# A hybrid mixer and mixture-of-experts layer on one core: ten tiles of the last norm finished through TensorE and ScalarE, the first tokens' numbers loaded by SyncE, five routing steps folded

## The chip, the cores and the metric

The kernel runs on one core of a Trainium2 chip. The metric is the device time of one execution in microseconds (us). A run's page and trace come from one profiled execution; the times in the result come from executions of the same program.

## What is computed

The reference is one layer over 2048 latent tokens (D = 1024) with 256 context tokens: adaLN, a projection, an mLSTM head group and an RWKV-7 head group in both directions, an output projection and a layer norm; then a mixture of experts, and a last layer norm. The change lies in the last two parts:

```python
x   = layernorm(ALPHA * x + g1 * (mixed @ w_out), ln1_g, ln1_b)
h   = modulate(x, sh2, sc2)                      # (2048, 1024)
# per token: best group of 4, best two of its 8 experts, softmax weights
y   = (silu(h @ ex_gate[e]) * (h @ ex_up[e])) @ ex_down[e]   # 32 experts, width 512
out = layernorm(ALPHA * x + g2 * ffn, ln2_g, ln2_b)
```

The last line is, for each token, `(x - mean) * rs * ln2_g + ln2_b`, where rs is one over the root of the variance plus 1e-6. All inputs and outputs are float32.

## The kernel before

The program is one TileContext. A planner simulates the program when it is built and fixes the order of the instructions on each engine from that simulation; on the chip every engine then runs its own list strictly in that order and waits where an operand is missing. `issue_after(ins)` (used with `with`) keeps the instructions of its block behind `ins`, on the engine of `ins` only.

**Output projection and routing** (`out_proj`, `route`, `route_end`). Sixteen tiles of 128 tokens are projected, normed and modulated; the modulated rows go to the DRAM tensor H2, the normed rows to ACC. The logits of the tiles are routed in batches of 4, 4, 3, 3, 1 and 1 tiles (`BATCHES`). `route` (line 1405 on) is a chain of small VectorE (DVE) instructions: the group's maximum, its number `gi` as the smallest index where the logit equals the maximum (an index minus 16, and plus 16 again at L1424), the same twice for the experts (an index minus 64, plus 64 at L1435; a one-hot row `e` at L1436, copied into the bfloat16 table `OH` at L1437), then the rank of each token within its expert by two TensorE products of `OH` with constant matrices, a place number `pos = expert * 2048 + rank` (L1461), cast to integers at L1463, and one indirect DMA of GpSimd (POOL) per tile and choice that writes token number and weight into the DRAM table TB (L1477): 32 scatters in all, ten of them in the last three batches.

**Experts** (`moe`). Every matrix of an expert is loaded as float32 in pieces (tile `eraw`, L1518, SyncE's queue) and split into a high part `eH` (ScalarE, L1531) and a rest `eL` (DVE, L1532: eraw minus eH), 12 pieces of 128x1024 per expert; the products run as three float32r matmuls each (L1565). `AHEAD = 8` pieces of the first expert are split before the tokens' numbers are asked for, two more (`W += ...`, line 1706) at the head of the loop over the 32 experts, the last two inside `gate_up`. Around the first tokens the order is:

- `load_ids(ids0, ...)`: a small DMA on POOL's queue (L1577) reads the numbers of the first 128 tokens of experts 0 and 1 from TB; it waits for all 32 scatters.
- `fetch` and `gather`: POOL's indirect DMAs (L1582) fetch the rows of H2: expert 0's tokens into `xg`, expert 1's into a tile of the weights' pool. The first weights of expert 1 wait for the second gather.
- `load_ids(t, ...)`: a second small DMA on POOL's queue loads the numbers for all experts into `yo`; POOL casts them (L1670).
- `split_T`: TensorE (PE) transposes `xg` (L1540), ScalarE takes the high part (L1548), DVE the rest (L1553); the last of these DVE instructions is `order`. Then PE transposes `t` in two halves (L1680), DVE copies each into `ids` (L1681), and expert 0's gate product begins.

The loop then runs 32 experts, adds each result into ACC with an accumulating scatter of POOL (L1651), and hands over to the last norm.

**Last norm** (`finish`). All 16 tiles of ACC are loaded (L1784). For tiles with m % 8 in (1, 3, 5, 6) ScalarE forms mean and variance with two passes (L1792, L1793), for the others DVE does (bn_stats, L75); DVE subtracts the mean and multiplies by ln2_g (L1796 or L1799), then multiplies by rs and adds ln2_b (L1800), both over 128x1024. The tile is stored from SyncE's queue (L1801).

Of the kernel before, what the change touches and what calls it, by code (L numbers as in the profile page):

```python
# [8 lines left out]
F = mybir.dt.float32  # L9
FR = mybir.dt.float32r  # L10
BF = mybir.dt.bfloat16
I32 = mybir.dt.int32
# [10 lines left out]
SEQ = 2048  # L23
# [15 lines left out]
def raw(ap, offset, dims):  # L39
    return bass.AP(tensor=ap.tensor, offset=ap.offset + offset, ap=dims)  # L40
# [13 lines left out]
class Kern:  # L54
# [4 lines left out]
    def pool(self, name, bufs, **k):  # L59

        if k.get("space") is not DRAM:
            k["reuse_waits"] = "tile"
        return self.tc.tile_pool(name=name, bufs=bufs, **k)
# [1313 lines left out]
    def route_consts(self, cp):  # L1377
        nc = self.nc
        c32 = cp.tile([128, 2, 32], I32, name="ci32")
        nc.gpsimd.iota(c32[:, 0, :], pattern=[[1, 32]], base=0, channel_multiplier=0)  # L1380
        nc.gpsimd.iota(c32[:, 1, :].rearrange("p (g e) -> p g e", e=8), pattern=[[1, 4], [0, 8]], base=0, channel_multiplier=0)
        self.i32 = cp.tile([128, 2, 32], F, name="cf32")
        nc.vector.tensor_copy(self.i32, c32)
        tk = cp.tile([128, 16], I32, name="tokid")
        nc.gpsimd.iota(tk, pattern=[[128, 16]], base=0, channel_multiplier=1)
        self.tokid = tk
        o = cp.tile([128, 128], F, name="onesf")
        nc.gpsimd.memset(o, 1.0)
        self.ones_b = cp.tile([128, 128], BF, name="ones_b")
        nc.vector.tensor_copy(self.ones_b, o)  # L1390
        nc.gpsimd.affine_select(out=o, in_=o, compare_op=OP.is_gt, fill=0.0, base=0, pattern=[[1, 128]],
                                channel_multiplier=-1)
        self.tri_b = cp.tile([128, 128], BF, name="tri_b")
        nc.vector.tensor_copy(self.tri_b, o)
        self.scat = []
        self.cnt = cp.tile([128, 32], F, name="cnt")
        nc.vector.memset(self.cnt, 0.0)
        self.OH = cp.tile([128, 16, 2, 32], BF, name="OH")
        self.rank = cp.tile([128, 16, 2], F, name="rank")
        self.keep = {}  # L1400
        for n2 in sorted(set(2 * n for _, n in BATCHES)):
            k = self.keep[n2] = cp.tile([128, 32, n2], F, name="keep%d" % n2)
            nc.vector.memset(k, 1.0)
            nc.vector.memset(k[:, :, 0:1], 0.0)

    def route(self, m0, n, L, rp, pp):
# [2 lines left out]
        bc = lambda a, w: a[:, :, None].to_broadcast([128, n, w])  # L1409
        row = lambda a: a[:, None, :].to_broadcast([128, n, a.shape[-1]])  # L1410
        lg, le = L[:, :, 0:4], L[:, :, 4:36]
        i32, grp = self.i32[:, 0, :], self.i32[:, 1, :]
        sm = rp.tile([128, 7, n], F, name="rsm%d" % n)
        gm, gi, i1, i2, v1, v2, pg = (sm[:, i, :] for i in range(7))
        b4 = rp.tile([128, n, 4], F, name="rw4%d" % n)
# [5 lines left out]
        nc.vector.tensor_scalar(b4, a4, 0.0, None, op0=OP.is_equal)  # L1421
        nc.vector.scalar_tensor_tensor(b4, b4, -16.0, row(i32[:, 0:4]), op0=OP.mult, op1=OP.add)
        nc.vector.tensor_reduce(gi, b4, axis=AX.X, op=OP.min)
        nc.vector.tensor_scalar(gi, gi, 16.0, None, op0=OP.add)  # L1424
        x = rp.tile(S, F, name="rx%d" % n)
        e = rp.tile(S, F, name="re%d" % n)
        nc.vector.tensor_tensor(e, row(grp), bc(gi, 32), op=OP.is_equal)
# [2 lines left out]
        for j, (v, i) in enumerate(((v1, i1), (v2, i2))):  # L1430
            nc.vector.tensor_reduce(v, x, axis=AX.X, op=OP.max)
            nc.vector.tensor_tensor(e, x, bc(v, 32), op=OP.is_equal)
            nc.vector.scalar_tensor_tensor(e, e, -64.0, row(i32), op0=OP.mult, op1=OP.add)
            nc.vector.tensor_reduce(i, e, axis=AX.X, op=OP.min)
            nc.vector.tensor_scalar(i, i, 64.0, None, op0=OP.add)  # L1435
            nc.vector.tensor_tensor(e, row(i32), bc(i, 32), op=OP.is_equal)  # L1436
            nc.vector.tensor_copy(self.OH[:, ms, j, :], e)  # L1437
            if j == 0:
                nc.vector.scalar_tensor_tensor(x, e, -2e30, x, op0=OP.mult, op1=OP.add)
        oh = self.OH[:, ms].rearrange("p i j e -> p (i j e)")  # L1440
        n2 = 2 * n
        ps = pp.tile([128, 2, n2, 32], F, name="rps")
# [17 lines left out]
        for j, i in enumerate((i1, i2)):  # L1460
            nc.vector.scalar_tensor_tensor(pos[:, :, j], i, float(SEQ), self.rank[:, ms, j], op0=OP.mult, op1=OP.add)  # L1461
        pi = rp.tile([128, n, 2], I32, name="rpi%d" % n)
        nc.vector.tensor_copy(pi, pos)  # L1463

        en = rp.tile([128, n, 2, 2], I32, name="ren%d" % n)
        nc.vector.tensor_copy(en[:, :, :, 0], self.tokid[:, ms][:, :, None].to_broadcast([128, n, 2]))
# [30 lines left out]
    def moe(self):  # L1497
        tc, nc, I, s = self.tc, self.nc, self.I, self.scratch
        with ExitStack() as es:
# [73 lines left out]
                                  mybir.DependencyInfo(mybir.DependencyClass.Sync, mybir.DependencyReason.DATA),  # L1573
                                  reason=reason)

            def load_ids(dst, src):
                ld = nc.gpsimd.dma_start(dst, src)  # L1577
                for sc in self.scat:
                    behind_dma(ld, sc, "entries of the token table")

# [76 lines left out]
                return x  # L1657

            Rs = {0: load_raw(0)}
            W = [split(Rs[0], i) for i in range(AHEAD)]  # L1660
            ids0 = ap.tile([128, 2, 2], I32, name="ids0", bufs=1)
            load_ids(ids0, raw(TBf, 0, [[2, 128], [2 * SEQ, 2], [1, 2]]))
            x0 = fetch(ids0[:, 0, 0:1])
            x = rawp.tile([128, 4, 512], F, name="eraw").rearrange("p k c -> p (k c)")[:, 0:D]
            self.first = gather(x, ids0[:, 1, 0:1])

            t = xp.tile([128, D], F, name="yo", bufs=1)[0:32, 0:768]
            load_ids(t.bitcast(I32), raw(TBf, 0, [[2 * SEQ, 32], [1, 768]]))
            t = t.rearrange("p (i w) -> p w i", w=2)
            nc.gpsimd.tensor_copy(t[:, 0], t[:, 0].bitcast(I32))  # L1670
            self.scat = []
# [25 lines left out]
            for e in range(NE):  # L1697
                nx, x1 = coming

                with behind():  # L1700
                    tc.mark_branch_hint_location("e%d" % e, hint=nx, engines=[PE])
                cur = ids[:, 0, e]
                act = bp.tile([128, DE], F, name="act")
                Aa = parts(bp, 4, "a")
                us = [pu.tile([128, 512], F, name="epu%d" % h) for h in range(2)]
                W += [split(Rs[e], i) for i in range(len(W), 10)]
                if left:
                    add(*left)
                with behind() if e == 0 else ExitStack():
                    gate_up(X, W, Rs[e])  # L1710
                last = self.pe

                def extra(i):


                    if not isinstance(i, int) or i > 1:
                        new = ap.tile([128, 2], I32, name="more")
                        load_ids(new, self.TB[bass.ds((i + (16 * e + 1)) * 128, 128), :])
                        gather(x1, new[:, 0:1])
                    else:  # L1720
                        new = ids[:, 1 + i, e]
                    old = ap.tile([128, 2], I32, name="old")
                    nc.vector.tensor_copy(old, cur)
                    nc.vector.tensor_copy(cur, new)
                    self.pe = None
                    Z = parts(xp, 8, "z")

                    def mid():
                        with tc.If(nx > 1):
                            gather(x1, ids[:, 2, e, 0:1])  # L1730

                    add(tail(W, lambda g: split_T(Z, x1, g, 4, later=g == 0), mid if isinstance(i, int) and i == 0 else None), old)
                    gate_up(Z, W)

                if e + 1 < NE:
                    coming = begin(e + 1, order)
                with tc.If(nx > 0, label="e%d" % e):  # L1737
                    tc.mark_branch_hint_location("f%d" % e, hint=nx - 1, engines=[PE])
                    extra(0)
                    with tc.If(nx > 1, label="f%d" % e):  # L1740
                        extra(1)
                        with tc.If(nx > 2):
                            with tc.For_i(2, nx, 1) as i:
                                extra(i)

                def fill(g):
                    nonlocal x
                    if e + 1 < NE:
                        late = split_T(X, x, g, 4, True, last, g == 0)
                    else:  # L1750
                        late = None
                    if g == 1 and e + 2 < NE:
                        x = fetch(ids[:, 0, e + 2, 0:1])
                    return late

                self.pe = None
                X = parts(xp, 8, "x")
                left = tail(W, fill), cur
                order = self.last
                if e + 2 < NE:  # L1760
                    Rs[e + 2] = load_raw(e + 2)
                if e + 1 < NE:
                    W = [split(Rs[e + 1], i) for i in range(2)]
                    with tc.issue_after(self.evac[0]), tc.issue_after(self.evac[1]):
                        W += [split(Rs[e + 1], i) for i in range(2, AHEAD)]
            add(*left)

    def finish(self):
        tc, nc, I = self.tc, self.nc, self.I
        with ExitStack() as es:  # L1770
# [2 lines left out]
            l2g, l2b = rows[:, 0], rows[:, 1]  # L1773
            for x, nm in ((l2g, "ln2_g"), (l2b, "ln2_b")):
                nc.scalar.dma_start(x, self.bcast_rows(flat(I[nm]), D))
            xp, tp = pool("fx", 8), pool("ft", 4)

            nc.scalar.activation(tp.tile([128, 1], F, name="fsq", bufs=1), self.eps_ln, AF.Sqrt)
            xs = []
# [5 lines left out]
            sq = tp.tile([128, D], F, name="fsc", bufs=1)  # L1785
            for m in range(16):
                x = xs[m]
                if m % 8 in (1, 3, 5, 6):

                    st = tp.tile([128, 4], F, name="fst")  # L1790
# [6 lines left out]
                else:  # L1797
                    mu, rs = self.ln_stats(tp, x, D, LN_EPS, "f")
                    nc.vector.scalar_tensor_tensor(x, x, mu, l2g, op0=OP.subtract, op1=OP.mult)  # L1799
                nc.vector.scalar_tensor_tensor(x, x, rs, l2b, op0=OP.mult, op1=OP.add)  # L1800
                nc.sync.dma_start(self.out[0, 128 * m:128 * m + 128], x)  # L1801

    def run(self, stop=None):
# [46 lines left out]
```

## Time and profile before

| | us |
|---|---|
| runs | 3412.34, 3418.94, 3422.70 (median 3418.94) |
| profiled execution, its own time | 3418.58 |
| its span, first to last instruction | 3417.0 |
| first gate product of expert 0 starts | 2306.65 |
| last product of the experts ends | 3351.4 |
| first and last DVE instruction of the last norm | 3361.99 and 3411.79 (ends 3413.07) |

Times in the rows are us from the start of the span. The execution's own time is 1.6 us longer than its span; the sum of the prediction is made against the execution's own time, 3418.58, which lies 0.36 us under the median. A row of the timeline view gives start, duration, engine, line, operation, written and read tiles, and in brackets how long the engine had been idle and what released it. DVE instructions overlap by some 0.1 us, so that the distance of two starts is the price of one in a row of them, not the duration. [...]

### The profile page before, as it was taken

To read this page: it belongs to the slowest core of one execution; us is meant where nothing else is said; L and a number is where in the kernel's file an instruction comes from. 1 tells how busy PE (TensorE), PEld (TensorE's weight loads), DVE (VectorE), ACT (ScalarE), POOL (GpSimd) and SP (SyncE) were. 2 spreads that over 40 slices of the span, in tenths; PEclk is the share of its full clock that TensorE was granted. 3 is DMA by queue.
4 is the path that set the end of the run, shared out by engine and by line. 5 is a ranking of instruction groups with operands and counts; after the bars stand their busy time and mean duration, and the time that the engine had idled before them with its cause. 6 is when DMAs were issued, how large, how long until landed. Compare 5 with 4: busy or idle time off the path is not lost. (4 is left out here: it accounts for less than half of the span.)

```text
span 3417.0 us, 61401 instructions
## 1 busy us (share of the span) xinstructions
PE 2866.9 (84%) x24042; PEld 2405.9 (70%) x24042; DVE 2339.6 (68%) x3822; ACT 1364.0 (40%) x2187; POOL 879.0 (26%) x862
## 2 busy tenths in 40 slices
PE   6899999999979964777777588859899989989992
PEld 3677788898757754666666567647778877878781
DVE  4488888766787875667656288875877736476447
ACT  4432322335545322334344233344655525355233
POOL 5400000013455660112112365431222212122210
PEclk9899999999979875778788789979999999999996
DMA  5333332235468534666664554448988848597535
GB/s 187 117 114 108 101 116 82 88 101 189 164 219 242 167 109 115 171 159 170 155 168 128 159 174 137 141 147 286 334 295 284 304 125 276 159 335 234 177 112 209
DMA packets 471689, 602.59 MB, mean 176 GB/s; under 512 B 127222, under 2 KB 312338, under 8 KB 471314
## 3 DMA queue, kind: packets, MB, share of 16 engines
q1 hardware_dynamic: 413617, 441.15, 41.2%
q0 software_dynamic: 36736, 129.33, 13.0%
q10 hardware_dynamic: 20960, 27.20, 2.5%
q8 instruction: 224, 3.67, 0.5%
q14 instruction: 152, 1.24, 0.1%
HBM read 453.24 MB, written 144.33 MB: 175 GB/s over the span
## 5 line engine op out<-in xcount | busy, mean ns | idle before, releaser
L1532 DVE TENSOR_TENSOR eL<-eraw,eH 128x1024 fp32r<-128x1024 f32 x384 | 449.6, 1221 | 28.6 <-ACT eH L1531 24.6
L329 DVE SCALAR_TENSOR_TENSOR cacc<-P,cw,cacc 128x1008 f32<-128x1008 f32 (+3 forms) x320 | 398.7, 1247 | 56.5 <-ACT cacc L304 45.6
L1531 ACT CAST eH<-eraw 128x1024 fp32r<-128x1024 f32 x384 | 370.9, 1052 | 48.3 <-PEq L1737 35.1
L263 PE MATMUL in_ps<-hH,w_H 128*128 128x512 f32 (+1 forms) x664 | 252.3, 382 | 1.7 <-ACT pl_ev L355 1.7
L263 PE MATMUL in_ps<-hL,w_H 128*128 128x512 f32 (+1 forms) x664 | 249.6, 377 | 0.0
L263 PE MATMUL in_ps<-hH,w_L 128*128 128x512 f32 (+1 forms) x664 | 248.0, 374 | 0.0
L1565 PE MATMUL epo<-eH,aH 128*128 128x512 f32 x408 | 172.2, 422 | 64.8 <-DVEq L1737 32.2
L1651 POOL DMA_INDIRECT ACC<-yo,ids x32 | 131.0, 4093 | 250.5 <-DVE yo L1650 226.1
L1565 PE MATMUL epo<-eH,aL 128*128 128x512 f32 x408 | 159.7, 404 | 11.7 <-DVE aL L1553 11.7
L1565 PE MATMUL epo<-eL,aH 128*128 128x512 f32 x408 | 163.2, 400 | 0.0
L931 PE MATMUL rpg<-KR,BK 64*128 64x128 f32 (+1 forms) x1152 | 122.4, 350 | 46.7 <-ACT BT L941 17.5
L237 POOL DMA_DIRECT2D w_raw<-in_w_in x28 | 21.2, 757 | 506.2 <-DVE w_L L251 371.8
L263 PEld LDWEIGHTS in_ps<-hH,w_H 128*128 128x128 f32 x664 | 126.2, 191 | 34.6 <-issue 11.5
L931 PEld LDWEIGHTS rpg<-KR,BK 64*128 64x128 f32 x1152 | 104.9, 248 | 63.2 <-issue 23.8
L973 DVE TENSOR_TENSOR sT<-sM,sY 128x31 f32<-128x31 f32 (+15 forms) x279 | 95.3, 342 | 78.8 <-DMA sM<-BL 70.8
L298 ACT COPY P<-in_ps 128x512 f32<-128x512 f32 (+1 forms) x92 | 51.3, 557 | 235.8 <-PE in_ps L263 235.8
L1565 PE MATMUL epu<-eH,xL 128*128 128x256 f32 x512 | 143.4, 283 | 0.0
L1565 PE MATMUL epu<-eL,xH 128*128 128x256 f32 x512 | 143.2, 283 | 0.0
L263 PEld LDWEIGHTS in_ps<-hL,w_H 128*128 128x128 f32 x664 | 126.2, 190 | 22.7 <-issue 2.1
L1565 PE MATMUL epu<-eH,xH 128*128 128x256 f32 x512 | 142.2, 288 | 0.0
L263 PEld LDWEIGHTS in_ps<-hH,w_L 128*128 128x128 f32 x664 | 126.1, 190 | 22.3 <-issue 0.8
L1565 PEld LDWEIGHTS epo<-eH,aH 128*128 128x128 f32 x408 | 78.9, 193 | 83.1 <-ACT xH L1548 30.7
(471 smaller groups left out, 8151.1 us busy)
## 6 DMA issues: line engine op xcount, KB each, us to landing
eraw<-in_ex_gate SPq DMA_DIRECT2D x64, 1024.0 KB
eraw<-in_ex_up SPq DMA_DIRECT2D x64, 1024.0 KB
eraw<-in_ex_down SPq DMA_DIRECT2D x64, 1024.0 KB
pk<-PK SPq DMA_DIRECT2D x144, 320.0 KB
PK<-pk POOLq DMA_DIRECT2D x36, 768.0 KB, 3.9
ada_w<-in_w_ada SPq DMA_DIRECT2D x32, 512.0 KB
v<-MV SPq DMA_DIRECT2D x50, 264.0 KB
kc<-KTd SPq DMA_DIRECT2D x50, 256.0 KB
```

What stands on the lines that cost most here:

```text
L237: self.wld = nc.gpsimd.dma_start(w[:, 4:8, o:o + cn], src[:, 4:8])
L263: nc.tensor.matmul(o, a[:, k, :], b, start=i == 0, stop=i == 3 * KT - 1)
L298: nc.scalar.copy(P[:, t0:t0 + n], ps)
L329: nc.vector.scalar_tensor_tensor(o, img[:, r0 + sy:r1 + sy, c0 + sx:c1 + sx], wt(dy, dx), o, op0=OP.mult, op1=OP.add)
L931: nc.tensor.matmul(pG[e][:, q, b.cols], b.BK[HD[e], c, q, :], b.KR[HD[e], c, q, b.cols], start=True, stop=True, tile_position=(64 * e, 0))
L973: nc.vector.tensor_tensor(tt, M[:, 0:j, j:j + 1].to_broadcast([128, j, w]), Y[:, j:j + 1, j:32].to_broadcast([128, j, w]), op=OP.mult)
L1531: self.cp = nc.scalar.copy(H, w)
L1532: nc.vector.tensor_tensor(L, w, H, op=OP.subtract)
L1565: self.pe = nc.tensor.matmul(o, a[:, k, :], b[:, kw, c], start=first and i == 0, stop=last and i == 2)
L1651: nc.gpsimd.indirect_dma_start(out=self.ACC, out_offset=bass.IndirectOffsetOnAxis(ap=cur[:, 0:1], axis=0), in_=y, in_offset=None, compute_ ...
```

## The change

Four edits. In `route` the indices stay at minus 16 and minus 64: the constants they are compared with are lowered by as much once (two more small DVE instructions in `route_consts`), the one-hot row is written straight into `OH`, and the place number is corrected by 64 * 2048 in the integer cast. So five DVE instructions of every batch go (one of L1424, two of L1435, two of L1437). In `moe` both `load_ids` before the loop go to SyncE's queue; only six pieces are split ahead, and the other four up to ten are traced at the head of the loop behind `order`, on DVE. In `finish`, for the ten tiles with m % 8 in (1, 2, 4, 5, 6), L1800 is replaced: POOL scales the identity by rs into `fdg` (128x128), PE adds the bias row as a product of a row of ones (`one`, K = 1) with ln2_b and the scaled tile as a product with `fdg`, per half of 512 columns, in one PSUM accumulation (tiles `fps`, three of them, two banks each), and ScalarE copies the 128x1024 sum to SBUF.

```diff
-        self.i32 = cp.tile([128, 2, 32], F, name="cf32")
-        nc.vector.tensor_copy(self.i32, c32)
+        self.i32 = cp.tile([128, 3, 32], F, name="cf32")
+        nc.vector.tensor_copy(self.i32[:, 0:2], c32)
+        nc.vector.tensor_scalar(self.i32[:, 2], self.i32[:, 0], -64.0, None, op0=OP.add)
+        nc.vector.tensor_scalar(self.i32[:, 1], self.i32[:, 1], -16.0, None, op0=OP.add)
...
-        nc.vector.tensor_scalar(gi, gi, 16.0, None, op0=OP.add)
...
-            nc.vector.tensor_scalar(i, i, 64.0, None, op0=OP.add)
-            nc.vector.tensor_tensor(e, row(i32), bc(i, 32), op=OP.is_equal)
-            nc.vector.tensor_copy(self.OH[:, ms, j, :], e)
+            o = self.OH[:, ms, j, :]
+            nc.vector.tensor_tensor(o, row(i64), bc(i, 32), op=OP.is_equal)
             if j == 0:
-                nc.vector.scalar_tensor_tensor(x, e, -2e30, x, op0=OP.mult, op1=OP.add)
+                nc.vector.scalar_tensor_tensor(x, o, -2e30, x, op0=OP.mult, op1=OP.add)
...
-        nc.vector.tensor_copy(pi, pos)
+        nc.vector.tensor_scalar(pi, pos, 64.0 * SEQ, None, op0=OP.add)
...
-            def load_ids(dst, src):
-                ld = nc.gpsimd.dma_start(dst, src)
+            def load_ids(dst, src, eng=nc.gpsimd):
+                ld = eng.dma_start(dst, src)
...
-            W = [split(Rs[0], i) for i in range(AHEAD)]
+            W = [split(Rs[0], i) for i in range(AHEAD - 2)]
...
-            load_ids(ids0, raw(TBf, 0, [[2, 128], [2 * SEQ, 2], [1, 2]]))
+            load_ids(ids0, raw(TBf, 0, [[2, 128], [2 * SEQ, 2], [1, 2]]), nc.sync)
...
-            load_ids(t.bitcast(I32), raw(TBf, 0, [[2 * SEQ, 32], [1, 768]]))
+            load_ids(t.bitcast(I32), raw(TBf, 0, [[2 * SEQ, 32], [1, 768]]), nc.sync)
...
-                W += [split(Rs[e], i) for i in range(len(W), 10)]
+                with tc.issue_after(order.ins) if e == 0 else ExitStack():
+                    W += [split(Rs[e], i) for i in range(len(W), 10)]
...
-            xp, tp = pool("fx", 8), pool("ft", 4)
+            xp, tp, pp = pool("fx", 8), pool("ft", 4), pool("fp", 3, space=PSUM)
+            one = tp.tile([1, 128], F, name="fone", bufs=1)
+            nc.vector.memset(one, 1.0)
...
+                last = m % 8 in (1, 2, 4, 5, 6)
...
-                nc.vector.scalar_tensor_tensor(x, x, rs, l2b, op0=OP.mult, op1=OP.add)
+                if last:
+                    dg = tp.tile([128, 128], F, name="fdg")
+                    nc.gpsimd.tensor_scalar(dg, self.ident, rs, None, op0=OP.mult)
+                    ps = pp.tile([128, 2, 512], F, name="fps")
+                    for h in range(2):
+                        c = slice(512 * h, 512 * h + 512)
+                        nc.tensor.matmul(ps[:, h], one, l2b[0:1, c], start=True, stop=False)
+                        nc.tensor.matmul(ps[:, h], dg, x[:, c], start=False, stop=True)
+                    nc.scalar.copy(x, ps.rearrange("p h c -> p (h c)"))
+                else:
+                    nc.vector.scalar_tensor_tensor(x, x, rs, l2b, op0=OP.mult, op1=OP.add)
```

## Rows read from the trace of the kernel before

**Rows 1.** The page, busy time of each engine over the whole span.

```profile
PE 2866.9 (84%) x24042; PEld 2405.9 (70%) x24042; DVE 2339.6 (68%) x3822; ACT 1364.0 (40%) x2187; POOL 879.0 (26%) x862
```

**Rows 2.** Stretches: length, PE, PEld, DVE, ACT, POOL busy, PE clock, DMA share, GB/s.

```profile
2306.60:2309.30 2.70, 2.65 (x6) 2.17 (x7) 0.19 (x1) 0.00 (x0) 0.17 (x1) 0.50 0.94 354
2309.30:2318.00 8.70, 8.70 (x57) 7.89 (x56) 0.22 (x1) 2.93 (x3) 1.72 (x2) 0.99 1.04 396
2318.00:3340.00 1022.00, 930.80 (x5385) 811.26 (x5384) 640.98 (x840) 471.05 (x621) 213.83 (x99) 0.98 0.74 240
...
3366.00:3413.00 47.00, 0.00 (x0) 0.00 (x0) 46.90 (x67) 20.05 (x43) 0.00 (x0) 0.50 0.74 300
```

**Rows 3.** The chain that ended last, the step into the last norm.

```profile
3359.80 6.25 DMA fx<-ACC
```

**Rows 4.** Timeline of the last norm, DVE.

```profile
3368.45 1.28 DVE L1796 SCALAR_TENSOR_TENSOR fx<-fx,fst,eraw 128x1024 f32<-128x1024 f32 x1
...
3369.65 0.16 DVE L1795 RECIPROCAL fst<-fst 128x1 f32<-128x1 f32 x1
...
3390.69 1.29 DVE L1800 SCALAR_TENSOR_TENSOR fx<-fx,fst,eraw 128x1024 f32<-128x1024 f32 x1
3391.89 1.29 DVE L1799 SCALAR_TENSOR_TENSOR fx<-fx,f_mv,eraw 128x1024 f32<-128x1024 f32 x1
...
3411.79 1.28 DVE L1800 SCALAR_TENSOR_TENSOR fx<-fx,f_mv,eraw 128x1024 f32<-128x1024 f32 x1
```

**Rows 5.** Timeline of PE in the output projection: float32 products (L1293), two others.

```profile
1956.38 2.05 PE L1293 MATMUL opo<-gB,sg 128*128 128x512 f32 x2 [11.83 <-DMA gB<-in_r_gB]
...
2047.77 1.02 PE L1293 MATMUL opo<-gB,sg 128*128 128x512 f32 x2
2048.63 0.60 PE L1347 MATMUL opt<-ident,t 128*128 128x128 f32 x4
...
2228.63 0.47 PE L1323 MATMUL opo<-woH,mH 128*128 128x512 f32 x1
...
2231.84 0.48 PE L1323 MATMUL opo<-woH,mL 128*128 128x512 f32 x1
```

**Rows 6.** Groups by line and shape over the span: nearest ScalarE and POOL instructions.

```profile
L1531 ACT CAST eH<-eraw 128x1024 fp32r<-128x1024 f32 x384 | 370.9, 1052 | 48.3 <-PEq L1737 35.1 <-DMA eraw<-in_ex_gate 5.3 <-DVE act L1622 2.7
...
L207 POOL TENSOR_SCALAR x<-x,hx_mv 128x1024 f32<-128x1024 f32 x16 | 61.0, 3816 | 26.2 <-DVE hx_mv L79 26.2
```

**Rows 7.** Timeline of POOL between the last scatter and the second gather.

```profile
2287.81 1.96 POOL L1477 DMA_INDIRECT TB<-ren,rpi  x1 [0.30 <-issue]
2291.61 0.77 POOL L1577 DMA_DIRECT2D ids<-TB  x1 [1.84 <-DMA TB<-ren,rpi]
...
2295.95 2.99 POOL L1582 DMA_INDIRECT xg<-H,ids  x1 [3.01 <-issue]
2299.25 0.96 POOL L1582 DMA_INDIRECT eraw<-H,ids  x1 [0.30 <-issue]
```

**Rows 8.** Timeline of DVE around the first tokens.

```profile
2275.69 0.17 DVE L1463 CAST rpi<-rpos 128x6 int32<-128x6 f32 x1
...
2286.52 11.50 DVE L1532 TENSOR_TENSOR eL<-eraw,eH 128x1024 fp32r<-128x1024 f32 x10
...
2305.64 0.23 DVE L1681 CAST ids<-ept 128x96 int32<-128x96 f32 x1
```

**Rows 9.** Timeline of PE around the first tokens.

```profile
2302.28 1.97 PE L1540 MATMUL ept<-ident,xg 128*128 128x128 f32 x8 [18.47 <-DMA xg<-H,ids]
...
2305.93 0.56 PE L1680 MATMUL ept<-ident,yo 32*128 32x32 f32 x3 [0.54 <-DVE ids L1681]
2306.65 0.79 PE L1565 MATMUL epg<-eH,xH 128*128 128x512 f32 x1 [0.16 <-issue]
```

**Rows 10.** Timelines of SyncE's queue and DVE: a 2 KB load and its first reader.

```profile
708.29 0.64 SPq L516 DMA_DIRECT2D gcel<-CF  x1
...
710.25 0.29 DVE L522 TENSOR_SCALAR gQ<-gQ,gcel 128x128 f32<-128x128 f32 x1
```

More of the change, by code (lines that the diff above doesn't have):

```diff
@@ L1411, in route @@
         lg, le = L[:, :, 0:4], L[:, :, 4:36]
-        i32, grp = self.i32[:, 0, :], self.i32[:, 1, :]
+        i32, grp, i64 = (self.i32[:, k, :] for k in range(3))
         sm = rp.tile([128, 7, n], F, name="rsm%d" % n)
```

## The prediction

> **What bounds the kernel now.** I first read the page for the shares [rows 1]: PE is busy 84% of the span, so a gain must be looked for where PE is not the bound. The table of stretches [rows 2] shows two such places next to the edits. In the last norm, 3366 to 3413, DVE is busy 46.90 of 47 us while PE and POOL do nothing, ScalarE works 20.05 us and the DMA engines 0.74 of the time: that stage is DVE's alone. The chain enters it through the loads of ACC [rows 3] and then stays on DVE until its last instruction ends at 3413.07 [rows 4]; the span closes 3.9 us later with the last store. The other place is the entry into the experts: between the last scatter and the first gate product, 2287.81 to 2306.65 [rows 7, 9], PE waits 18.47 us for the first tokens. What lies between, the 32 experts, is PE's (930.80 of 1022 us), so an earlier start there should be carried to its end.
>
> **Edit 1, the last norm.** Removed: ten of sixteen L1800 passes. One lasts 1.29 us, but start to start it is 1.20 (3390.69 to 3391.89) [rows 4]. Ten are 12.0 us; DVE alone would end at 3413.07 - 12.0 = 3401.1. The memset of `one` is one small instruction before the stage, while DVE waits for the loads: nothing; if that cover went, some 0.2 us.
>
> Added on PE: four float32 products of 512 columns per tile. One such product is two matmuls; the pair that starts at 2047.77 is drawn as 1.02 us, but what follows starts at 2048.63, so in a row of them a product costs 0.86 us at full clock [rows 5]. Right behind 11.83 us of idling the same pair took 2.05 us [rows 5], twice as long: 1.71 in a row at half clock. Forty products are 34 us. Six of them, the bias rows of the first three tiles, need neither the tile nor rs, only a free PSUM tile, and there are three: the planner pulls ready matmuls ahead of ones that wait, as it did with the products of mH, issued at 2228.63 and the ones of mL of the same sum only at 2231.84 [rows 5]. So I let 34 products count from the first scaled tile. That is m = 1: its L1796 starts at 3368.45, its rs is ready at 3369.81 [rows 4], and POOL's 128x128 scaling is an eighth of 3816 ns [rows 6], 0.5 us; POOL is idle there, so only this latency counts. PE begins at 3370.3 and needs 34 x 0.86 = 29.2 us: 3399.5.
>
> To that come two losses. The granted clock is at 0.50 in this stretch, after PE's last product at 3351.4. At the entry into the experts PE ran 2.7 us of dense matmuls, 7.0 us from its first transpose, before the clock went from 0.50 to 0.99 [rows 2, 9]; half clock for 2.7 to 7.0 us loses 1.4 to 3.5 us, and I take 2.0, near the dense case. [...] Second, tiles reach PE unevenly (m = 4, 5, 6 close together, then two tiles that are not its own); between 0 and 5 us of idling I take 2.0. So PE ends at 3403.5.
>
> ScalarE then copies 128x1024 out of PSUM; the nearest row is its cast of that size, 1052 ns [rows 6]; below nothing it can't be, twice that is the upper bound. Ten are 10.5 us on 20.05, 31 of the 38 us left, so it isn't the bound by load. With 0.1 us before and after, the last copy ends at 3404.7, after DVE's 3401.1. **PE, not DVE, sets the end.** The store's tail of 3.9 us stays: 3408.6 against 3417.0, **-8.4 us**. Bounds: DVE alone, -12; and about -1, below.
>
> Each copy queues on ScalarE in front of later tiles' statistics and square roots, for which DVE waits. If the planner thinks PE faster than it is, each copy stands there too early and both engines wait: that is the first rival.
>
> **Edit 2, the first tokens.** The load of the numbers is issued on POOL at 2291.61, and the gather that needs them starts at 2295.95 [rows 7]: 4.34 us. The nearest load from SyncE's queue has the same 2 KB over 128 partitions: issued at 708.29, first reader at 710.25 [rows 10], 1.96 us. The new one moves twice as many runs (two of 8 bytes per partition), so I take 2.2: **-2.1**; bounds 1.96 and 4.34, or -2.4 to 0. SyncE's queue has nothing else to do then: what follows, expert 1's weights, waits for the second gather anyway. The second load is moved with it and stays beside this path. [...]
>
> Six pieces instead of ten ahead: the first gather takes 2.99 us where the second takes 0.96 [rows 7]. DVE's row of ten L1532 ends at 2298.02 [rows 8]; 0.96 behind that is 2298.98, and the gather ended at 2298.94. So the gather stood until DVE's two-input subtractions stopped. [...] Six pieces are 6.9 us and end at about 2293, as the gather becomes ready: **-2.0**; bounds 0 and -2.03.
>
> The four late pieces stand behind `order` on DVE, and the first copy into `ids` comes right after it, at 2305.64 [rows 8]. PE's second half of the transposes waits for that copy, and the gate product for it [rows 9]. The first late piece is ready at once, the copy only after PE's first half; I expect one piece, 1.15 us, in between: **+1.1**; bounds 0 and two pieces, +2.3. The up products need these pieces 7 us later (2306.65 to 2313.6), so the rest is hidden.
>
> **Edit 3, routing.** Five small DVE instructions per batch go, each about as long as the cast at 2275.69, 0.17 us [rows 8]. Only the last batches count: that cast releases the last ten scatters, which run on POOL without a pause, 1.3 us each, to the one at 2287.81 [rows 7]. Five less in front of the cast are worth 0.85 us at most where DVE waits for each result, half of that where they overlap; some of the next batch's stand in front too, so I take **-0.6**; bounds 0 and ten of them, -1.7. The last batches' own chains shorten as well, so they don't take over. The two new constants cost 0.2 us of DVE once, far ahead.
>
> **Sum.** -2.1 - 2.0 + 1.1 - 0.6 = -3.6 at the entry, -8.4 at the end: -12.0. 3418.58 - 12.0 = 3406.6; the median lies 0.36 higher, so 3406.9. A measurement of this kernel tells about 0.3% from no change, 10.3 us.
>
> **Rivals.**
>
> *The order on ScalarE gives back most of edit 1.* For it: queues are strict, PE is at half clock just when the first copies are due, and DVE reads every rs after a ScalarE root. If all forty products ran after 3370.3 and PE idled 5 us, the stage would end at 3370.3 + 34.4 + 2 + 5 + 1.2 = 3412.9, nearly as before. Against it: PE has six products of head start. Time: between that and the forecast, -4 + -3.6, some 3411. Chance 0.27.
>
> *PE stays at half clock through the last norm: slower.* Place: from 3370.3; price: 34 x 1.71 = 58.1 us instead of 29.2, so the last copy ends at 3429.6, +16.5, or with the entry +12.9: 3431.8. It decides if the gaps between PE's bursts keep the clock at 0.50. Against it: work at half clock outruns its supply, so there would be no gaps, and at the entry 2.7 us of dense work were enough [rows 2]. Chance 0.05.
>
> *The numbers land no sooner from SyncE.* Then edit 2 gives -0.1 - 2.0 + 1.1 and the sum is -10.0: 3408.9. Against it stands the 1.96 us load [rows 10]. Chance 0.13.
>
> *The earlier start is lost among the experts* (their weights come late instead: the DMA share is 1.04 in 2309 to 2318 [rows 2]): -8.4 alone, 3410.5. Against it: those loads start with the second gather, which moves too. Chance 0.05.
>
> **How the numbers follow.** The forecast has 0.50. Its own range is from -12 and -5 to -6 and -2: 3402 to 3411. Taking in the first rival's upper part gives 3401.5 to 3415.5; what is left out is the slow rival, the worst of the first, and luck below. Faster by over 0.3% (under 3408.7) is most of the forecast, 0.44, nearly half of the third rival, 0.06, and a little of the first, 0.06: 0.56. Slower is the second rival, 0.05. The rest, 0.39, is within 0.3%.
>
> **What would show it.** L1800 six times; PE matmuls at L1809 or so with pairs 0.43 apart after a first tile at 0.85; DVE's last pass near 3398 and the last ScalarE copy behind it; ScalarE waiting for PE in the waits. At the entry: the first gather 0.96 long and some 4.7 us earlier, a piece between `order` and the first copy into `ids`, the gate product near 2303. It is wrong if DVE idles over 3 us in the last norm, if PE's clock there stays at 0.50, or if the gather still lasts 3 us.

## The result and the profile after

The changed kernel takes 3445.09 us (median of five runs, 3435.66 to 3450.34) against 3418.94: ratio 1.0072, 95% interval 1.0052 to 1.0092. It is slower, and the time lies outside the predicted range. The profiled execution of after took 3449.26 us (span 3447.6), 30.7 over the one of before.

Four marks cut both traces into stretches: the start of the last row of router products (opl), the start of the last scatter, the first gate product, the end of the last expert product. The same marks serve all runs below (us; the kernels are explained with the experiments).

| kernel | opl to last scatter | last scatter to gate | gate to last expert product | to the end |
|---|---|---|---|---|
| before | 13.92 | 18.84 | 1044.7 | 65.6 |
| after | 14.04 | 21.80 | 1044.5 | 84.8 |
| after, 128-row bias products | 14.04 | 22.28 | 1048.4 | 64.4 |
| after, no bias products | 13.22 | 22.50 | 1042.6 | 60.0 |
| after, eight tiles, one-row bias | 14.06 | 21.83 | 1051.4 | 77.3 |
| after, late pieces behind the copies | 14.06 | 17.94 | 1052.7 | 84.7 |
| after, numbers loaded by GpSimd | 14.00 | 21.23 | 1043.4 | 91.0 |
| after, load cut in two | 13.02 | 20.64 | 1054.4 | 90.3 |
| after, g2 rows later | 14.03 | 19.33 | 1052.5 | 88.2 |
| after, old last norm (three traces) | 13.01, 14.04, 14.01 | 22.33, 22.00, 21.94 | 1046.4, 1050.5, 1046.1 | 64.7, 64.9, 65.6 |
| before again (two traces) | 13.91, 13.91 | 18.77, 18.81 | 1051.4, 1043.7 | 65.5, 65.4 |
| before with the new norm (eight tiles, 128 rows) | 13.91 | 18.83 | 1043.4 | 57.9 |
| combined, first version | 13.98 | 17.28 | 1047.8 | 57.1 |
| combined, five pieces held | 13.94 | 17.47 | 1050.0 | 56.9 |
| combined, SyncE in two loads, g2 later | 13.26 | 15.62 | 1049.5 | 59.9 |

Of the 30.6 us between the two spans, 19.2 lie behind the last expert product and 3.0 between last scatter and gate. 8.6 more lie ahead of the last row of router products, some 7 of them before any line that the change touches. Over the traces of the table that point wanders by 13 us (2269.15 to 2282.45), and by 7.8 us among four traces in which nothing ahead of it is changed, so this part is taken for variation between executions. The two real losses, 22 us, fit the ratio, whose interval is 18 to 31 us.

The last norm first. Stretches of after (length, PE, PEld, DVE, ACT, POOL busy, PE clock as a share of full speed, DMA share, GB/s): the whole tail, its middle, then PE from its first scaled product to its last, and three shorter pieces.

```profile
3362.40:3447.60 85.20, 65.46 (x82) 18.29 (x80) 39.80 (x65) 31.61 (x58) 11.59 (x11) 0.62 0.54 203
3397.00:3432.00 35.00, 35.00 (x37) 9.80 (x37) 15.96 (x25) 8.69 (x17) 5.40 (x4) 0.50 0.32 130
3382.00:3442.80 60.80, 60.79 (x74) 16.96 (x74) 30.96 (x50) 24.55 (x45) 9.43 (x9) 0.61 0.50 202
...
3382.00:3387.00 5.00, 4.99 (x5) 1.50 (x6) 5.00 (x10) 4.82 (x11) 1.63 (x1) 0.50 1.03 410
3387.00:3392.00 5.00, 5.00 (x9) 1.56 (x8) 5.00 (x7) 3.81 (x7) 1.19 (x2) 0.80 1.03 410
3437.00:3442.00 5.00, 5.00 (x11) 1.48 (x10) 0.00 (x0) 1.01 (x1) 0.00 (x0) 1.00 0.51 210
```

In before DVE was busy 46.90 of 47 us here and PE did nothing [rows 2]. Now PE is busy without a gap, 35.00 of 35.00 us in the middle, at a clock of 0.50, while DVE works 15.96. The chain that ended last says the same (start, length, engine, tile, line; two matmuls are one product):

```profile
3382.01 2.07 PE fps L1813 x2
3384.08 2.00 PE fps L1812 x2
3386.08 3.37 PE fps L1813 x4
3389.45 1.05 PE fps L1812 x2
...
3392.70 2.01 PE fps L1813 x2
...
3402.42 2.01 PE fps L1813 x2
3404.43 2.00 PE fps L1812 x2
...
3440.71 1.05 PE fps L1812 x2
3441.76 1.07 PE fps L1813 x2
3442.85 1.01 ACT fx L1814
```

L1812 is the bias product, L1813 the scaled one. Each costs 2.00 us at half clock (0.50) and 1.05 at full clock (1.00) when the two alternate. The clock rose near 3389, was back at half from 3392.7 on, and rose again only near 3433; PE had no idle time in between. From the first scaled tile to the last ScalarE copy nothing but PE stands on the chain. The groups by line of the tail show who waits:

```profile
L1813 PE MATMUL fps<-fx,fdg 128*128 128x512 f32 x40 | 34.0, 968 | 13.9 <-POOL fdg L1808 13.9
L1812 PE MATMUL fps<-eraw,fone 1*128 1x512 f32 x40 | 33.1, 940 | 1.0 <-issue 1.0
L1814 ACT COPY fx<-fps 128x1024 f32<-128x1024 f32 x10 | 10.1, 1010 | 36.1 <-PE fps L1813 36.1
L79 DVE RECIPROCAL f_mv<-f_mv 128x1 f32<-128x1 f32 x8 | 1.2, 153 | 6.2 <-ACT f_mv L78 6.2
```

ScalarE stands 36.1 us in front of its copies, and DVE 6.2 us for a root that is queued behind such a copy. Note the shape in the second row: `1*128`, one row of operands, where the first has 128.

The entry into the experts, timeline of after (start, length, engine, line, operation; in brackets the idle time before it and what ended it):

```profile
2294.20 1.99 POOL L1478 DMA_INDIRECT TB<-ren,rpi  x1 [0.80 <-DVE rpos L1462]
2296.49 1.97 POOL L1478 DMA_INDIRECT TB<-ren,rpi  x1 [0.30 <-issue]
2299.82 0.37 SPq L1578 DMA_DIRECT2D ids<-TB  x1
2299.86 0.36 ACTq L1207 DMA_DIRECT2D g2b<-modd  x1
2305.29 1.01 POOL L1583 DMA_INDIRECT xg<-H,ids  x1 [6.83 <-issue]
2309.61 1.97 PE L1541 MATMUL ept<-ident,xg 128*128 128x128 f32 x8 [18.25 <-DMA xg<-H,ids]
2312.90 4.61 DVE L1533 TENSOR_TENSOR eL<-eraw,eH 128x1024 fp32r<-128x1024 f32 x4
2317.51 0.24 DVE L1682 CAST ids<-ept 128x96 int32<-128x96 f32 x1
2317.80 0.56 PE L1681 MATMUL ept<-ident,yo 32*128 32x32 f32 x3 [5.08 <-DVE ids L1682]
2318.29 0.80 PE L1566 MATMUL epg<-eH,xH 128*128 128x512 f32 x1
```

Against [rows 7 to 9]: the gather takes 1.01 us instead of 2.99, as predicted. From the issue of the load of the numbers to the gather pass 5.47 us instead of 4.34. All four late pieces stand on DVE ahead of the first copy into `ids`, and PE waits 5.08 us for that copy, so transposes to gate are 8.68 us instead of 4.37. The last scatter but one, issued 0.05 us behind the start of DVE's pieces (2294.20 for 2294.15), takes 1.99 us. In before it took 0.96, though it came as close behind them (2286.55 for 2286.52 [rows 8]); why that one was short is open.

### The profile page after: what moved, and what is told of

Read it like the earlier page. It is cut to its first block, busy times and chain, and to the rows that moved or that the text cites. A ratio compares the mean times of both kernels' runs of the same rounds, so it can differ in the third digit from the quotient of the medians.

```text
span 3447.6 us, 61550 instructions
## 1 busy us (share of the span) xinstructions
PE 2937.8 (85%) x24122; PEld 2429.0 (70%) x24122; DVE 2332.3 (68%) x3785; ACT 1374.6 (40%) x2197; POOL 889.8 (26%) x870
```

## Experiments

**Does the depth of the bias product hold the clock?** The changed kernel with the one-row operands made 128 rows deep:

```diff
-            one = tp.tile([1, 128], F, name="fone", bufs=1)
-            nc.vector.memset(one, 1.0)
+            one = tp.tile([128, 128], F, name="fone", bufs=1)
+            nc.vector.memset(one, 1.0 / 128)
...
-                        nc.tensor.matmul(ps[:, h], one, l2b[0:1, c], start=True, stop=False)
+                        nc.tensor.matmul(ps[:, h], one, l2b[:, c], start=True, stop=False)
```

> The changed kernel, with only the bias product's operands made 128 rows deep (a tile of 1/128 against all 128 copies of the bias row, the same sum); the number of matmuls and their columns stay. Theory A, it is the products with a one-row operand that leave TensorE at half clock although it never idles: the clock of the last norm goes to 1.00 soon after the products of the first tiles, a pair then takes 0.86 to 1.05 us instead of 2.0, and last expert product to end falls from 84.8 us to 57 to 64; the kernel's time falls by 20 to 28 us. Theory B, float32 products of this stage hold the clock at half whatever the depth of their operands: clock .50, 84.8 us within 2, no change of the time.

Stretches of that run, the tail and its middle:

```profile
3362.90:3427.30 64.40, 38.94 (x81) 16.01 (x80) 38.97 (x65) 31.27 (x58) 11.78 (x11) 0.86 0.71 269
3385.00:3405.00 20.00, 19.49 (x45) 8.24 (x44) 20.00 (x37) 18.42 (x36) 4.01 (x5) 0.98 0.86 345
```

The same matmuls with the same columns, and the clock is 0.98 in the middle instead of 0.50. The tail falls by 20.4 us to 64.4, just above theory A's upper end. Timed: 3428.96 us, 16 less than the changed kernel where 20 to 28 were expected; the ratio to before is 1.0016, interval 1.0000 to 1.0031. Theory B falls.

But 64.4 is only 1.2 us less than before, where the forecast had 8.4. The timeline of this run shows what is late now:

```profile
3407.93 2.78 POOL L1808 TENSOR_SCALAR fdg<-ident,f_mv 128x128 f32<-128x128 f32 x2 [11.79 <-DVE f_mv L79]
3409.44 2.00 PE L1813 MATMUL fps<-fx,fdg 128*128 128x512 f32 x2 [3.51 <-POOL fdg L1808]
3411.78 1.28 DVE L1816 SCALAR_TENSOR_TENSOR fx<-fx,f_mv,eraw 128x1024 f32<-128x1024 f32 x1
3420.68 1.02 PE L1812 MATMUL fps<-eraw,fone 128*128 128x512 f32 x2
3421.54 1.02 PE L1813 MATMUL fps<-fx,fdg 128*128 128x512 f32 x2
3422.60 1.01 ACT L1814 COPY fx<-fps 128x1024 f32<-128x1024 f32 x1 [2.42 <-PE fps L1813]
```

DVE's last pass ends at 3413.06, 50.1 us behind the last expert product (61.7 in before): DVE did gain nearly its 12 us (11.6). But PE idled 3.5 us and then got its last four tiles only from 3409.44 on, so the end is PE's burst at the finish and one copy, 10.5 us after DVE. That is the first rival's kind of loss, an order in which the engines come one behind the other, with a late DVE reciprocal, for which POOL's scaling of these tiles had waited 11.79 us, in place of ScalarE's copies as the late link. (Two products in a row start 0.86 us apart here, 3420.68 to 3421.54.)

**Without bias products** (the last norm's bias is left out for ten tiles):

> The changed kernel without the bias products (the last norm's bias is left out for ten tiles): twenty float32 products instead of forty. Theory A (one-row products leave the clock at half): the clock rises to 1.00 behind the first tile or two, and the tail from the last expert product to the end is about as long as in the run with 128-row bias products, or shorter, 54 to 58 us, set by VectorE's 34.9 us and ScalarE. Theory B (such products run at half clock whatever the operands): 20 x 1.71 = 34 us of TensorE at .50 from about 3370, so the tail is 84.8 - 34 + a few us of waits, 52 to 60 us, with the clock still at .50. The clock in the windows tells the two apart, not the time.

```profile
3347.50:3407.50 60.00, 22.01 (x40) 8.51 (x40) 38.94 (x65) 30.99 (x58) 12.48 (x11) 0.74 0.76 289
3372.00:3383.00 11.00, 8.43 (x20) 3.18 (x18) 11.00 (x18) 10.93 (x22) 2.38 (x4) 1.00 1.03 414
```

The clock reaches 1.00 in the middle of the tail with 77% busy time, where the changed kernel stayed at 0.50 with 100%. As theory A had it; the tail, 60.0, is longer than its 54 to 58, again by the late last tiles.

**Is it the choice of tiles?** Eight tiles on TensorE, the last five tiles left to DVE, one-row products kept (`last = m in (1, 2, 4, 5, 6, 8, 9, 10)`):

> The changed kernel with eight tiles on TensorE as in the combined version, but with the one-row bias products kept. Theory A (the one-row products hold the clock at half): the windows of the last norm show mostly .50, 26 products at 1.71 us from about 19 us behind the last expert product set the end, tail 68 to 78 us. Theory B (it was the five late tiles, and the clock only followed from them): full clock from the fourth tile on, tail 57 to 60 us as in the combined version.

```profile
3363.50:3440.80 77.30, 57.42 (x64) 16.22 (x64) 41.72 (x67) 29.59 (x56) 10.95 (x9) 0.54 0.59 224
3394.00:3436.00 42.00, 41.98 (x44) 11.34 (x42) 22.06 (x33) 12.58 (x24) 5.37 (x3) 0.50 0.45 180
```

Half clock over 42 us without a gap, 77.3 us: theory A. The tiles alone don't mend it. Both together, put into the kernel before with nothing else changed:

> The kernel before with only the last norm of the combined version (eight tiles on TensorE, 128-row bias products); entry and routing as before. Theory: the tail is that of the combined version within 1 us and the entry stays 18.84 within 0.3, so the time is 7 to 10 us under the kernel before; the combined version is 1 to 2 us better than this one, which a timing can't tell. Rival, this tail is no shorter than 65.6: then the time is that of the kernel before.

```profile
3355.50:3413.40 57.90, 30.54 (x65) 12.39 (x64) 41.37 (x67) 29.09 (x56) 10.78 (x9) 0.84 0.79 299
3380.00:3406.00 26.00, 22.33 (x51) 9.14 (x49) 26.00 (x40) 17.71 (x33) 6.99 (x6) 1.00 0.80 322
...
3406.40:3411.40 5.00, 0.00 (x0) 0.00 (x0) 1.10 (x1) 0.00 (x0) 0.00 (x0) 0.73 1.01 406
```

The tail is 57.9 us, 7.7 less than before; in the 26 us shown DVE has no gap and PE runs at full clock. Timed: 3410.06 us, ratio 0.9971, interval 0.9955 to 0.9987. In the five us of the last row the DMA engines are the busy ones (share 1.01).

**The other two edits alone**, the changed kernel with the old last norm:

> The changed kernel with the last norm as it was before; the other two edits stay. Theory: the whole loss is in the last norm and the entry nets a loss of 2 to 4 us: last expert product to end is 65.6 us within 1 (84.8 in the changed kernel), last scatter to first gate product 21.8 within 0.5, and the time is 0 to 5 us above that of the kernel before, not to be told from it. Rival: the other edits cost something outside these stretches (the 6.8 us by which the profiled execution was late before any changed code), then the time stays 6 to 12 us above the kernel before.

Ratio 1.0025, interval 1.0009 to 1.0041 (3429.6 us): the tail is back at 64.7, the entry stays long, and the kernel is slower than before, not the same: 3429.6 against 3422.23, 7.4 us, which lies in the rival's range of 6 to 12. Routing and entry explain 2.6 to 3.3 us of it in the three traces (the first two columns of the table against before). The interval reaches down to 3.1 us, so more than that isn't shown. To see whether the experts take longer behind this entry, two more traces of each kernel came from one chip:

> The kernel before once more, for a second trace of it on one chip beside the changed entry. Theory 1, the 32 experts take what the execution happens to give: first gate product to last expert product 1043 to 1054 us here too, as in the other traces, and no shorter than beside the changed entry. Theory 2, the changed entry costs the experts 4 us or more: this stretch is at least 4 us shorter here than in both traces of the changed entry of this set.

> The changed kernel with the last norm of before (entry and routing changed), again, beside the kernel before on one chip. Theory 1: experts within the spread of the two traces of the kernel before, entry 22.3 us within 0.5, tail 65 within 1. Theory 2: experts at least 4 us longer than in both of those.

The experts took 1051.4 and 1043.7 us in the kernel before, 1050.5 and 1046.1 behind the changed entry: theory 1. The entry is the steady difference, 18.77 and 18.81 against 22.00 and 21.94.

**The late pieces.** Only their place on DVE changes (`idc` is the last copy into `ids`):

```diff
-                with tc.issue_after(order.ins) if e == 0 else ExitStack():
+                with tc.issue_after(idc.ins) if e == 0 else ExitStack():
```

> The changed kernel, but the four late weight pieces are put behind the second copy of the token numbers instead of behind the order point. If the late pieces in front of that copy are what lengthened the way from the first transpose to the gate product: 8.68 us falls to 4.2 to 4.6 us, the copy follows the last split of the tokens within 0.5 us, and nothing is lost before the up products are through (first gate product to last expert product stays 1044.5 within 1.5). Rival: the up products now wait for the pieces, and 2 us or more of the gain is given back between the gate product and the expert's end.

```profile
2304.07 1.97 PE L1541 MATMUL ept<-ident,xg 128*128 128x128 f32 x8 [18.28 <-DMA xg<-H,ids]
2307.42 0.23 DVE L1682 CAST ids<-ept 128x96 int32<-128x96 f32 x1
2308.85 0.79 PE L1566 MATMUL epg<-eH,xH 128*128 128x512 f32 x1
2309.13 4.62 DVE L1533 TENSOR_TENSOR eL<-eraw,eH 128x1024 fp32r<-128x1024 f32 x4
```

Transposes to gate: 4.78 us instead of 8.68, just above the expected 4.2 to 4.6. The pieces cost 3.9 us there. Whether any of it is given back later can't be read from the experts' 1052.7 us: with the pieces left as in the change that stretch took 1042.6 to 1054.4.

**The load of the numbers.** Three variants of the changed kernel: GpSimd issues it; SyncE issues it in two loads of 128 numbers; SyncE issues it as in the change, but the 512 KB of g2 rows come behind the gathers.

> The changed kernel with both loads of the token numbers issued by GpSimd again, as in the kernel before; the six pieces ahead stay. If the load from SyncE is the slower one here (5.47 us from its issue to the start of the gather, against 4.34 from GpSimd): 4.3 to 4.6 us, from the last scatter to the gather 8.0 to 8.3 us instead of 8.80, and the gather stays 1.0 us long since VectorE's row of pieces ends before it. Rival, the 5.47 us come from the load of the g2 rows that starts at the same moment, whichever queue the numbers take: then 5.3 us or more from GpSimd too.

> The changed kernel with the load of the first two blocks' numbers from SyncE cut in two, the first block's 128 numbers ahead, the second's in a load of its own. In the changed kernel SyncE's queue moved 320 packets in the 5.5 us between the issue and the gather, where GpSimd's moved 64 for the same two loads. If the number of small packets makes it slower: 128 packets instead of 256 stand in front of the gather, and issue to gather falls from 5.47 to 4.2 to 4.9 us. Rival, the load of the g2 rows issued at the same moment makes it slower: 5.2 to 5.7 us as before.

> The changed kernel with the 512 KB load of the g2 rows moved behind the second gather, so that it no longer runs beside the load of the numbers. If that load's company makes the numbers late: issue to gather falls from 5.47 to 2.2 to 4 us (the load of 2 KB from SyncE at 708 was read after 1.96). Rival, the 256 small packets do: 5.2 us or more still.

The issue and the gather in each, first from GpSimd:

```profile
2289.45 0.77 POOL L1578 DMA_DIRECT2D ids<-TB  x1 [1.84 <-DMA TB<-ren,rpi]
...
2293.82 1.05 POOL L1583 DMA_INDIRECT xg<-H,ids  x1 [3.04 <-issue]
```

in two loads:

```profile
2293.94 0.81 SPq L1578 DMA_DIRECT2D ids<-TB  x2
...
2296.88 1.00 POOL L1583 DMA_INDIRECT xg<-H,ids  x1 [6.14 <-issue]
```

with the g2 rows later:

```profile
2291.97 0.37 SPq L1576 DMA_DIRECT2D ids<-TB  x1
...
2294.88 1.01 POOL L1581 DMA_INDIRECT xg<-H,ids  x1 [4.32 <-DMA ids<-TB]
```

4.37, 2.94 and 2.91 us, where the change has 5.47 (5.45 to 5.58 in eight traces). The queues show what differs. First the kernel before, from the issue to the gather (queue, packets, MB, share of 16 engines), then after:

```profile
q0 software_dynamic: 64, 0.10, 9.8%
```

```profile
q1 hardware_dynamic: 320, 0.10, 7.7%
```

The same two loads are 64 packets from GpSimd's queue and 320 from SyncE's. With the g2 rows later SyncE's 320 are the only ones, and 288 of them are under 512 bytes; 256 of these are, by an estimate from the first load's shape (128 partitions, two runs of 8 bytes each), its runs. 256 runs without the g2 rows take 2.91, 128 beside the g2 rows 2.94, and only 256 beside the g2 rows 5.5. So neither theory holds by itself; in these single traces it takes the two together. With both changes made (the last variant below) it is 2.52, little less. (The last norm is the changed one in these three, with tails of 88.2 to 91.0.)

**A combined version**: 128-row products, eight tiles, late pieces behind the copies, numbers from GpSimd.

> The changed kernel with what the runs so far show: 128-row bias products, numbers loaded by GpSimd, late pieces behind the copies of the numbers, and eight tiles on TensorE instead of ten, the last five tiles wholly on VectorE. Theory: the last PE products no longer come behind VectorE's last pass, so the last norm is VectorE's again with eight passes less (9.6 us): last expert product to end 56 to 58 us (65.6 before), last scatter to first gate product 17.2 to 17.8 (18.84 before); 8 to 11 us under the kernel before. Rival, the statistics and copies on ScalarE make VectorE wait instead: tail 60 to 65 us, and the time 2 to 6 us under the kernel before, not to be told from it.

Tail 57.1, entry 17.28, both in the expected range; 3414.11 us, ratio 0.9974, interval 0.9957 to 0.9991. Two more variants:

> The combined version with five pieces ahead instead of six, and VectorE's first piece held until the last scatter but one has landed. Theory: the last two scatters take 0.96 us each instead of 1.98 and 1.97, the gather stays at 1.0 us, so that the gate product comes 2 us earlier against the last router product (opl); from the first of the last eight opl products' last row to the last scatter 13.0 instead of 13.98 us, last scatter to gate 16.2 to 16.6 instead of 17.28; tail 57 within 1. The time is some 2 us under the combined version, 10 under the kernel before. Rival, five pieces end behind the ready gather and hold it up, so that less than 1 us is left.

> The combined version with the numbers loaded by SyncE after all, in two loads of 128 packets and with the g2 rows behind the gather. Theory: issue to gather 2.9 us (4.37 from GpSimd, 5.5 in the changed kernel), so last scatter to first gate product 15.2 to 16.5 us against 17.28 in the first combined version and 18.84 before; tail 57 within 1; the time 8 to 12 us under the kernel before. Rival, the saving is taken back by a later landing of the scatters, as in the run with the split load, where 3.20 us lay between the last scatter and the issue: then 17 to 18 us.

Holding the pieces made the last two scatters 0.96 us long, but the first of them started 1.2 us behind its cast instead of 0.3 (why, the trace doesn't say), and nothing was won: entry 17.47, ratio 0.9979 (0.9962 to 0.9996). With SyncE's two loads the entry is 15.62, 3.2 us under before, but the tail is 59.9 where 57 was expected (why is open): 0.9982 (0.9967 to 0.9997). These and the norm alone (0.9971) can't be told apart. The simplest of them, the norm alone, is the one to keep; 2 to 3 us at the entry are lost in runs of one kernel that spread over more than 20 us.

## Why the prediction was wrong

**The step that failed is the clock in edit 1.** The forecast let half clock cost 2.0 us. It stayed for most of the tail (a mean of 0.61 over PE's 60.8 us), and making the bias operands 128 rows deep, which took PE to full clock, shortened the tail by 20.4 us. The second rival had the right place and nearly the right price (the last copy 16.5 us later; the tail grew by 19.2). The price was near by luck: it took 1.71 us for every product, where one cost 2.00 at half clock and 1.05 in the parts at full clock. And its condition, "if the gaps between PE's bursts keep the clock at 0.50", was the wrong one, as was the argument against it: "work at half clock outruns its supply, so there would be no gaps". There were no gaps, and the clock was 0.50. The row at the entry that seemed to show 2.7 us to be enough [rows 2] was of products 128 rows deep; half of the new ones have one row, and the first experiment and the two versions with eight tiles show that this decides. (The 2.7 us were short even for deep products: in after the same gate products ran from 2318.3 to 2324.0, 5.7 us, at 0.50.) No run has a long row of one-row products alone, so whether they do it by themselves or only in alternation with deep ones isn't shown. That gaps of PE brought its clock down here the trace does not show: the clock fell again near 3392 (1.00 from 3391 to 3392, 0.50 from 3393 to 3394) with PE busy 1.00 of each us, and it stayed at 0.50 with PE 35.00 of 35.00 us busy; with 128-row operands in the same place it was 0.98.

**The price of a product** is right where its conditions held: 0.86 us at full clock in the run with 128 rows. The one-row mix cost 1.05 at full and 2.00 at half, not 0.86 and 1.71.

**Gaps and order.** The term "between 0 and 5 us of idling I take 2.0" and the first rival were about the right trouble: with the clock mended the gain was 1.2 us instead of 8.4, since the last four tiles reached PE only 3.6 us before DVE was done. With eight tiles, the last five left to DVE, it was 7.7. Right were DVE's 12 us (11.6) and the copy of 1.01 us (1.05 forecast). The head start was half of what the sum took:

```profile
3363.84 4.24 PE L1812 MATMUL fps<-eraw,fone 1*128 1x512 f32 x6 [1.02 <-issue]
```

Two matmuls are one product, so three bias products ran ahead of the first tile instead of six, and 37 were left instead of 34: 2.6 us more at full clock.

**Edit 2.** The gather: -1.98 for a forecast of -2.0. It starts 4.25 us behind the end of DVE's pieces (2301.04). POOL's scaling of `fdg` in the last norm of after differs in the same way: 0.60 to 0.61 us beside DVE's statistics, which read one tile, or with DVE idle, and 1.63, 2.57 and 1.64 us where it starts beside a two-input pass of DVE. The load: "I take 2.2" from a load of 2 KB that ran in other company; it took 5.47, so +1.1 for -2.1, beyond the bound that I had set at 0. This is the place of the third rival, whose -0.1 (the gap of two issues, 0.77 and 0.64 us [rows 7, 10]) no run shows: from SyncE the gather started 1.1 us later than the 4.34 of before beside the g2 rows (5.47), and 1.4 us sooner without them (2.91). Nor was 4.34 a fixed price of the old load: in four traces of that entry the gather starts 4.30 to 5.05 us behind the issue, but ends 7.33 to 7.35 behind it in each, as it would if DVE's pieces set its end. In after it ends 6.48 behind it, so load and gather together gained 0.9 of 4.1 us. The late pieces: "I expect one piece, 1.15 us, in between" was +1.1; four stood there, +4.3 (3.9 of them given back when the pieces were moved), beyond the bound of two. Nothing in the code limits them to one: `order` only says what they come behind.

**Edit 3.** The cast that counts is that of the last batch, in front of the last two scatters (at 2286.12 in before); the one at 2275.69, which the forecast took for all ten, is 128x6 and serves six. The last one comes 0.9 us earlier (11.3 us behind the start of the last router products for 12.2), a little more than the 0.6; but in eight of the fourteen traces with the changed routing it is lost again: the last scatter but one took 1.98 to 1.99 us for 0.96. With DVE's pieces held until it had landed it took 0.96; in the other five it took 0.95 to 0.96 too.

**Sum.** Entry and routing +3.1 for -3.6, last norm +19.2 for -8.4. That an entry is carried through the experts could be neither shown nor refuted, since they vary by 12 us between executions.

## What to carry to other kernels

A product priced at full clock needs a row at full clock with operands of the same depth (here 0.86 us with 128 rows, and 1.05 or 2.00 in the mix with one-row products): ask of each new PE instruction what clock rows like it ran at, and of a bias added as a one-row product whether 128 rows, which cost no more here (0.86 us a product), keep PE at full clock (0.98 for 0.50 here). When work is ordered only "behind" a point, count all of it ahead of the next thing on that engine. A load's price comes from a row with the same runs and the same company (the same 2 KB took 2.91 or 5.47 us); count the packets that its queue makes of it (64 or 320 here).

## What the runs showed of the hardware

One-row float32 products, alternating with 128-row ones, left TensorE at 0.50 for over 40 us without an idle gap, though not all the time: in the changed kernel it reached 1.00 for some 3 us on the way and again for the last 9 us of PE's work. With 128 rows in their place, or with none, it was at 0.98 to 1.00 in the middle of the same stage. The 2 KB load of 8-byte runs and the 96 KB load behind it were 320 packets from SyncE and 64 from GpSimd; the gather followed the issue of the first after 5.5 us from SyncE beside a 512 KB load, after 2.9 from SyncE without it, and after 4.4 from GpSimd beside it.
